# Attention by whole heads on 128 rows, and a first stage that alternates x and weights by K tile

## The chip, the cores and the metric

The kernel runs on one core of a Trainium2 chip. The metric is the device time of one execution in microseconds. A core has TensorE (PE: matmuls and transposes; its weight loads are listed apart as PEld), VectorE (DVE), ScalarE (ACT), GpSimd (POOL), SyncE (SP, which here only issues transfers), DMA queues that the engines issue into, an SBUF of 128 partitions and a PSUM of eight banks, each of 128 partitions by 512 floats, for matmul results.

## The reference

A decoder trunk of two layers on one sequence of 256 tokens, 2048 wide, everything in float32. Each layer projects the normed input to q, k, v (1024 columns each) and three 1024-column inputs of a gated convolution, runs differential attention over 8 heads beside the convolution, projects both back, and ends with a squared-ReLU MLP of 8192 columns.

```
for l in range(DEPTH):
    h = _rmsnorm(x, attn_norm_g[l])
    q, k, v, gate_b, gate_c, conv_in = jnp.split(h @ w_in[l], splits, axis=-1)
    q = _rmsnorm(q.reshape(B, S, N_HEADS, 2, HEAD_DK), q_norm_g[l])
    k = _rmsnorm(k.reshape(B, S, N_HEADS, 2, HEAD_DK), k_norm_g[l])
    ...
    s = jnp.einsum('bqhmd,bkhmd->bhmqk', q, k) * scale + bias
    s = jnp.where(dist >= 0, s, NEG)
    p = jax.nn.softmax(s, axis=-1)
    p = p[:, :, 0] - lam * p[:, :, 1]
    attn = jnp.einsum('bhqk,bkhd->bqhd', p, v)
    attn = (_rmsnorm(attn, subln_g[l]) * (1.0 - lam_init)).reshape(B, S, ATTN_WIDTH)
    conv = gate_b * _short_conv(gate_c * conv_in, conv_w[l])
    x = x + jnp.concatenate([attn, conv], axis=-1) @ w_out[l]
    hm = _rmsnorm(x, mlp_norm_g[l]) @ w_up[l]
    x = x + jnp.square(jax.nn.relu(hm)) @ w_down[l]
```

A head has two score maps (m = 0, 1), each over 64 of its 128 q and k columns. The maps are softmaxed apart and combined with a factor lambda.

## The kernel before

**Precision.** Every float32 matrix product is made of three products in the type fp32r: each operand is split into a rounded part `hi` and a rest `lo`, and `TERMS` (L38) lists hi x hi, hi x lo and lo x hi. The splits are made on ACT (`hi`, a copy that rounds) and DVE (`lo`, a subtraction). Transposes go through TensorE against an identity `ident`, in plain fp32.

**Stages.** A layer is a *mixer* (L602 to L664) and an *mlp* (L670 to L985). The tokens are two tiles t of 128. In the mixer come, for each half of the heads (four heads, 512 columns), three calls of `linear` (L328) named q, k and v; then eight calls of `linear_t` (L347) named gc and ci in turns, four named gb, and four calls of `linear` named o. `linear` runs over 16 K tiles (128 rows of weights each), with six matmuls of 128x128 by 512 columns a K tile (two token tiles by three terms). `linear_t` holds weights as the stationary operand. A group of four K tiles takes eight matmuls of 512 columns, activations' hi and lo side by side against the weights' hi, and eight of 256 against their lo.

**Weights.** `Weights` (L268) is a queue of jobs in program order. A job loads a piece of two K tiles (512 KB, issued on SP) into a `raw` tile, and `halves` rounds it: `whi` on ACT (L285), `wlo` on DVE (L286). There are four `raw` tiles and three pairs of rounded ones (`wpool`). `take` (L313) hands the next piece to TensorE and has made three jobs more by then (`AHEAD`). In layer 0 the first two pieces are rounded by K tile (`cut`). For layer 0, `first_loads` (L989) issues two weight loads ahead of each further part of x; the four parts of x are named x0 to x3 in what follows, each 512 columns of all 256 tokens, and the weight pieces w0, w1 and on. x0 is loaded in two halves at the very start (L146).

**Order of work.** TensorE's order is the program's, written out by hand (L116). The other engines' instructions are put in order by a scheduler when the kernel is built; only those given to `late` (L118) keep the program's order. Work beside the stages comes from `Background` (L55): generators that give a number with each yield, namely after how many ticks they go on. A tick is one K tile of `linear` (six matmuls of 512 columns), or four matmuls of 512 or four of 256 in `linear_t`. When a generator goes on, its TensorE instructions are put in TensorE's order at that place.

**Norms.** `Norm.chunk` (L397) transposes one of the four parts of x (16 transposes in two PSUM banks), multiplies by the gain and splits (`split_gained`, L249), marks the part ready, and squares x with a running sum. `Norm.factors` (L420) makes the row factors, which multiply the projections afterwards, and `across`, the same factors spread along columns by a matmul (`rbc`, L446), for the convolution. The generators of layer 0 are started at ticks 1, 5 and 9 of the first q pass; the first part is done ahead of it.

**q and k.** `qk_norm` (L458), started when a pass ends, squares and norms the result on ACT, DVE and POOL, waits 8 ticks (L477), transposes each token tile (four heads, a bank) and writes hi and lo of all heads in one ACT and one DVE instruction each (L484, L485), a tick apart.

**Attention.** `attention` (L489), started 3 ticks after a v pass, runs one `unit` for each token tile and head, tile 0 first, staggered by 4 ticks (L573). So attention of heads 0 to 3 runs beside the q pass of the second half, and that of heads 4 to 7 beside gc and ci. A unit makes two score maps, three matmuls each with 64 rows of contraction (L503) and 128 (t = 0) or 256 (t = 1) key columns; adds the bias and takes the maximum on DVE (L506); exponentials with sums on ACT (L513); combines the maps into `p` on DVE (L524); 9 ticks later transposes `p` (L529), splits it into `pT` (L531, L532); and 4 ticks later multiplies by v (L539, 3 or 6 matmuls of 128 columns) into one bank `av` for four heads. The last unit of a token tile copies that bank, norms it, waits 9 ticks (L562) and transposes it into `dst`, the input of o. `s` has three buffers, `p` and `pT` two each, in the pool `tmp` (L606).

**Bias.** `load_bias` (L230) starts at tick 10. In layer 0 it first runs `small_setup` (L199), which turns small vectors (loaded at L168 to L183 by POOL's queue) into gains and factors, and writes the biases by distance to DRAM; two 1 MB loads then read them back with a shift for each row (L238), and after 4 ticks (L241) eight ACT copies (L244) mirror them into `bias`. 

**Memory.** `nat` (L111) holds work tiles of 512 columns, seven of them; `bpool` (L608) holds eight tiles of 2048 columns: q, k and v parts, bias loads, attention and convolution outputs; `fill` (L131) is a tile that nothing uses, and sets where the ones behind it lie.

Of the kernel before, what the change touches and what calls it, by code (L numbers as in the profile page):

```python
# [15 lines left out]
P = 128  # L16
# [5 lines left out]
NH = 8  # L22
# [79 lines left out]
def trunk(ctx: ExitStack, tc: tile.TileContext, x, w_in, w_out, conv_w, q_norm_g, k_norm_g,  # L102
# [8 lines left out]
    nat = ctx.enter_context(tc.tile_pool(name="nat", bufs=7))  # L111
# [19 lines left out]
    const.tile([P, 40], F32, tag="fill", name="fill")  # L131
# [4 lines left out]
    def load_x(n, cuts=1):  # L136
        for c in range(cuts):
            lo, hi = c * CH // cuts, (c + 1) * CH // cuts
            nc.sync.dma_start(
                xs[n][:, :, lo:hi],  # L140
                x[0, :, n * CH + lo:n * CH + hi].rearrange("(t p) c -> p t c", p=P))
# [4 lines left out]
    load_x(0, 2)  # L146
# [3 lines left out]
    mhalf = const.tile([P, NH], F32, tag="mhalf", name="mhalf")  # L150
    nc.vector.memset(mhalf, -0.5)
# [16 lines left out]
    vec = const.tile([ROWS, P], F32, tag="vec", name="vec")  # L168
    nc.gpsimd.dma_start(vec[0:NCW, :], conv_w.rearrange("l i (k p) -> (l i k) p", p=P))
    for i, g in enumerate((q_norm_g, k_norm_g)):  # L170
        for m in range(2):
            nc.gpsimd.dma_start(
                vec[QG + i * DEPTH:QG + (i + 1) * DEPTH, m * DK:(m + 1) * DK], g)
    nc.gpsimd.dma_start(vec[QG + 2 * DEPTH:MG, :], subln_g)
    nc.gpsimd.dma_start(vec[MG:ROWS, :], mlp_norm_g.rearrange("l (k p) -> (l k) p", p=P))
    lamv = const.tile([1, 4, DEPTH, DK], F32, tag="lamv", name="lamv")
    for i, a in enumerate((lambda_q1, lambda_q2, lambda_k1, lambda_k2)):
        nc.gpsimd.dma_start(lamv[:, i], a[None])
    sel = const.tile([NB + 1, REL], F32, tag="sel", name="sel")
    nc.gpsimd.dma_start(sel, selector)  # L180
    rel = const.tile([NB + 1, 2 * NH], F32, tag="rel", name="rel")
    nc.vector.memset(rel[NB:NB + 1, :], NEG)
    nc.gpsimd.dma_start(rel[0:NB, :], rel_bias)  # L183
    ones = const.tile([P, P], F32, tag="ones", name="ones")
    nc.vector.memset(ones, 1.0)

# [12 lines left out]
    def small_setup():  # L199
# [27 lines left out]
        nc.vector.tensor_copy(nlam, lps[:, :DEPTH])  # L227


    def load_bias(l, bpool, bias):  # L230

        if l == 0:
            yield from small_setup()
# [154 lines left out]
    class Norm:  # L388
# [31 lines left out]
        def factors(self):  # L420
            while not all(t.ready for t in self.tiles):
                yield 1
# [607 lines left out]
```

## Time and profile before

| | |
|---|---|
| median of three runs | 2178.3 us (2177.54 to 2178.63) |
| the profiled execution | 2181.2 us, its span 2179.4 us |
| TensorE | 11066 instructions |
| VectorE | 2229 instructions |
| ScalarE | 1718 instructions |
| GpSimd | 194 instructions |
| read from HBM, written | 425.84 MB, 18.90 MB |
| MLP's share of the chain of waits | upc 29%, dn 15%, pr 13% |
| mixer's share | o 8%; q, k, v, gc, ci, gb 4% each; sc 1%, av 1% |

The page comes from one profiled execution. Busy time of an engine is the sum of its instructions without overlap; TensorE's matmuls are pipelined, so that the duration shown for one (0.39 us for 512 columns) is longer than the distance of two starts (0.227 us). In the chain of waits each step leads back from the end of the kernel to what released it, or to the instruction ahead of it on its engine. In a table by stretches each row has the stretch in us, its length, the busy time and instruction count of TensorE, its weight loads, VectorE, ScalarE and GpSimd, the TensorE clock that was granted (1.00 is full), the DMA engines' busy share, and GB/s. In rows of the timeline and of the chain come the start in us, the length, the engine, the source line, and the destination and sources by the program's names; `x6` is a run of six instructions, and square brackets hold the idle time ahead and what ended it.

### The profile page before, as it was taken

What the parts mean: (1) busy time and instruction counts of PE and PEld (TensorE: products, weight loads), DVE (VectorE), ACT (ScalarE), POOL (GpSimd) and SP (SyncE); (2) the same over time, 40 slices, a digit from 0 to 9 for tenths busy, and PEclk for the clock granted to TensorE, in tenths of its full rate; (3) what the DMA queues carried; (4) which work ended last, traced back from release to release, by engine and by line L of the source; (5) the groups of instructions that cost most, each with busy time, mean ns of one, the idle gap of its engine ahead of it and who ended that gap; (6) DMA issues with size and microseconds to landing.
All of it is one profiled execution on the core that took longest, in us unless ns stands there. A gap on an engine that the chain in (4) does not pass through costs nothing.

```text
span 2179.4 us, 29050 instructions
## 1 busy us (share of the span) xinstructions
PE 2156.3 (99%) x11066; PEld 1828.2 (84%) x11066; DVE 1604.7 (74%) x2229; ACT 1271.6 (58%) x1718; POOL 136.9 (6%) x194
## 2 busy tenths in 40 slices
PE   8999999999999999999999999999999999999999
PEld 6888888888888888888888888888888888888887
DVE  6677655698888888855566776557988888887554
ACT  6456445566666666644455664446666666665443
POOL 2021100000000000100011111000000000001000
PEclk9999999999999999999999999999999999999999
DMA  7545666476666666577565465656676666666774
GB/s 261 177 154 188 209 184 189 158 242 212 215 217 217 211 213 218 192 265 241 174 212 175 155 210 190 188 166 198 218 219 216 213 213 216 218 209 211 246 241 145
DMA packets 292491, 446.62 MB, mean 205 GB/s; under 512 B 10403, under 2 KB 191221, under 8 KB 292352
## 3 DMA queue, kind: packets, MB, share of 16 engines
q1 hardware_dynamic: 285648, 423.66, 61.4%
q0 software_dynamic: 6656, 21.10, 2.6%
q8 instruction: 86, 1.41, 0.3%
q14 instruction: 53, 0.43, 0.1%
q10 hardware_dynamic: 48, 0.02, 0.0%
HBM read 425.84 MB, written 18.90 MB: 204 GB/s over the span
## 4 chain that ended last, share of the span: by engine, by line
PE 94%; DVE 2%; DMA 2%; ACT 1%; issue 1%; SPq 0%; DVEq 0%; ACTq 0%
PE upc L812 29%; PE dn L972 15%; PE pr L852 13%; PE o L341 8%; PE q L341 4%; PE gc L363 4%; PE ci L363 4%; PE k L341 4%; PE gb L363 4%; PE v L341 4%; PE upw L812 1%; DMA uraw<-in_w_up_dram 1%; PE sc L503 1%; PE av L539 1%; DVE ulo L698 1%
## 5 line engine op out<-in xcount | busy, mean ns | idle before, releaser
L286 DVE TENSOR_TENSOR wlo<-raw,whi 128x1024 fp32r<-128x1024 f32 (+1 forms) x386 | 474.3, 1230 | 383.5 <-ACT whi L285 379.4
L285 ACT ACTIVATE whi<-raw 128x1024 fp32r<-128x1024 f32 (+1 forms) x386 | 406.8, 1055 | 477.6 <-PE dn L972 167.0
L812 PE MATMUL upc<-nT,uhi 128*128 128x512 f32 x1920 | 477.6, 391 | 0.0
L697 ACT ACTIVATE uhi<-uraw 128x1024 fp32r<-128x1024 f32 x256 | 271.0, 1060 | 285.7 <-PE upc L812 254.0
L812 PEld LDWEIGHTS upc<-nT,uhi 128*128 128x128 f32 x1920 | 352.8, 188 | 68.2
L698 DVE TENSOR_TENSOR ulo<-uraw,uhi 128x1024 fp32r<-128x1024 f32 x256 | 312.9, 1222 | 115.5 <-ACT uhi L697 113.1
L972 PE MATMUL dn<-whi,g 128*128 128x512 f32 x1024 | 316.4, 389 | 0.0
L812 PEld LDWEIGHTS upc<-nT,ulo 128*128 128x128 f32 x1920 | 261.9, 190 | 18.7
L812 PE MATMUL upc<-nT,ulo 128*128 128x256 f32 x1920 | 267.7, 282 | 0.0
L972 PEld LDWEIGHTS dn<-whi,g 128*128 128x128 f32 x1024 | 192.2, 188 | 39.7
L972 PE MATMUL dn<-wlo,g 128*128 128x512 f32 x512 | 199.7, 390 | 1.2 <-DVE wlo L286 1.0
L341 PE MATMUL o<-whi,cat 128*128 128x512 f32 x512 | 159.6, 390 | 0.0
L972 PEld LDWEIGHTS dn<-wlo,g 128*128 128x128 f32 x512 | 96.1, 188 | 22.9 <-DVE wlo L286 2.9
L341 PEld LDWEIGHTS o<-whi,cat 128*128 128x128 f32 x512 | 96.1, 188 | 19.8
L341 PE MATMUL o<-wlo,cat 128*128 128x512 f32 x256 | 99.6, 389 | 0.0
L834 POOL DMA_DIRECT2D hid<-h x64 | 35.0, 546 | 950.0 <-ACT h L833 914.1
L852 PE MATMUL pr<-t13h,f 128*128 128x512 f32 x240 | 93.8, 391 | 0.0
L341 PE MATMUL q<-whi,nT 128*128 128x512 f32 x256 | 86.2, 406 | 3.6 <-ACT nT L251 3.6
L341 PE MATMUL k<-whi,nT 128*128 128x512 f32 x256 | 85.3, 399 | 0.0
L852 PE MATMUL pr<-t24h,f 128*128 128x512 f32 x240 | 84.0, 391 | 0.0
L852 PE MATMUL pr<-b2h,f 128*128 128x512 f32 x240 | 84.0, 391 | 0.0
L341 PE MATMUL v<-whi,nT 128*128 128x512 f32 x256 | 83.4, 396 | 0.0
(330 smaller groups left out, 3428.5 us busy)
## 6 DMA issues: line engine op xcount, KB each, us to landing
uraw<-in_w_up_dram SPq DMA_DIRECT2D x128, 1024.0 KB, 5.9
raw<-in_w_in_dram SPq DMA_DIRECT2D x192, 512.0 KB, 3.9
draw<-in_w_down_dram SPq DMA_DIRECT2D x64, 1024.0 KB, 5.0
raw<-in_w_down_dram SPq DMA_DIRECT2D x64, 1024.0 KB, 5.3
raw<-in_w_out_dram SPq DMA_DIRECT2D x64, 512.0 KB, 3.6
hid<-h POOLq DMA_DIRECT2D x64, 256.0 KB, 4.3
back<-hid SPq DMA_DIRECT2D x32, 512.0 KB, 3.3
rev<-by_dist_d POOLq DMA_DIRECT2D x4, 1024.0 KB, 10.1
```

The source lines that it names most:

```text
L285: nc.scalar.activation(hi[:, k], raw[:, k], AF.Copy)
L286: nc.vector.tensor_sub(lo[:, k], raw[:, k], hi[:, k].bitcast(F32))
L341: nc.tensor.matmul(acc[:, t], a.ap[:, pa, k % KG, t * P:(t + 1) * P], (hi, lo)[pw][:, j], start=(k == 0 and n == 0), stop=(k == nk - 1 and ...
L363: nc.tensor.matmul(acc[:, f, 0] if part else acc[:, f], wt[:, k % 4, fs], a.ap[:, 0, k % KG] if part else a.ap[:, :, k % KG], start=(part ...
L503: nc.tensor.matmul(sc[:, :W], qT[m * DK:(m + 1) * DK, a, i, t * P:(t + 1) * P], kT[m * DK:(m + 1) * DK, b, i, :W], start=(n == 0), stop=(n ...
L539: nc.tensor.matmul(av[:, i * P:(i + 1) * P], pT[:, a, k * P:(k + 1) * P], v[:, b, k, i * P:(i + 1) * P], start=(k == 0 and n == 0), stop=( ...
L697: nc.scalar.activation(hi, src, AF.Copy)
L698: nc.vector.tensor_sub(lo, src, hi.bitcast(F32))
L812: nc.tensor.matmul(acc[:, 0] if part else acc, wt[:, k], a.ap[:, 0, k % KG] if part else a.ap[:, :, k % KG], start=(part == 0 and kh == 0 ...
L834: nc.gpsimd.dma_start(hid[i // 2][:, i % 2 * 2 * S:(i % 2 + 1) * 2 * S], u)
L852: nc.tensor.matmul(prods[n], fs[j][:, pa, a], b[pw], start=(j == 0 and m == 0), stop=(stop and m == 2))
L972: nc.tensor.matmul(acc[:, t], f[:, pa, k, t * P:(t + 1) * P], (hi, lo)[pw][:, k % 2], start=(b == 0 and k == 0 and m == 0), stop=(b == NB2 ...
```

## The change

**Attention.** A unit takes one head with both token tiles, and units are staggered by 8 ticks. Its two score maps go into two banks. Scores contract 128 rows: `q_parts` puts q's hi on a map's 64 rows and q's lo on the other 64; `k_parts` puts k's hi on both halves (`kT`) and k's lo on the map's rows with zeros on the others (`kL`, zeroed by POOL at the start of a mixer). One matmul with `kT` gives hi x hi + lo x hi, one with `kL` hi x lo. So a head has four matmuls of 128 columns and four of 256, all with 128 rows, where it had twelve with 64. The parts are written by 64-row halves: two ACT and two DVE instructions a token tile for q (one and one before), and four ACT and two DVE ones for k. The three blocks of a head's `p` are transposed one after the other, and `pT` hi multiplies v's hi and lo side by side (256 columns), `pT` lo v's hi (128 columns): six matmuls for nine. The halves of `av` are added, and the result squared, head by head. `s` holds both tiles (two buffers, and `p` is written in place of its first map); `pT` has one buffer. The waits are 10 ticks for 9 ahead of p's transposes, 12 for 9 ahead of the output's, 12 for 8 ahead of q's and k's.

**Start.** `begin` loads, on SP, half of x0 (256 KB), K tile 0 of w0 (256 KB), the other half of x0, K tile 1, then w1, x1, w2, w3, x2, x3. `Norm.begin` takes the K tiles of x0 one by one: two transposes, the split, and the rounding of that K tile's weights (of w0 and w1). TensorE runs matmuls of a tile of ones ahead of that, 11 at first and 3 after every second K tile, in plain fp32, whose result nothing reads. In layer 0 the squares of x1 and x2 come 10 and 8 ticks after their transposes, so the row factors (and `rbc`) come in the k pass. `take` makes one job ahead at first and up to three later, and the first roundings keep the program's order.

**Setup and bias.** The small vectors go to a tile of `bpool`, `setup_loads` issues them at the beginning of layer 0's mixer, and in layer 0 the bias copies wait 12 ticks for 4. `nat` has six tiles for seven, `fill` 48 columns for 40, and some small tiles have one buffer.

```
@@ -128,27 +128,36 @@
...
-    load_x(0, 2)
...
+    ones = const.tile([P, P], F32, tag="ones", name="ones")
+    nc.vector.memset(ones, 1.0)
...
+    def warm_up(n):
+
+        for _ in range(n):
+            nc.tensor.matmul(warm[:, 0, :P], ones, ones, start=True, stop=True)
...
     ident = const.tile([P, P], F32, tag="ident", name="ident")
     make_identity(nc, ident)
-    mhalf = const.tile([P, NH], F32, tag="mhalf", name="mhalf")
-    nc.vector.memset(mhalf, -0.5)
+    warm_up(11)
...
@@ -274,19 +289,42 @@
...
-            first = self.cut and i < 2
-            for k in (slice(0, 1), slice(1, None)) if first else (slice(None),):
-                nc.scalar.activation(hi[:, k], raw[:, k], AF.Copy)
-                nc.vector.tensor_sub(lo[:, k], raw[:, k], hi[:, k].bitcast(F32))
+            if not self.by_tile:
+                pair = (nc.scalar.activation(hi, raw, AF.Copy),
+                        nc.vector.tensor_sub(lo, raw, hi.bitcast(F32)))
+                if self.ramp and len(self.made) < 7:
+                    for ins in pair:
+                        late(ins)
...
+        def begin(self):
...
+            self.by_tile = self.ramp = True
+            raw = self.pool.tile([P, 2, CH], F32, tag="raw", name="raw", bufs=RAW)
+            w, row, c = self.first
+            for k in range(2):
+                load_x(0, k * CH // 2, (k + 1) * CH // 2)
+                nc.sync.dma_start(raw[:, k], w[row + k * P:row + (k + 1) * P, c:c + CH])
+            self.early.append(raw)
+            self.load_early(1)
+            raws = list(self.early)
+            self.made += [self.jobs[i]() for i in range(2)]
+            self.by_tile = False
+
+            def part(k):
+                (hi, lo), raw, j = self.made[k // 2], raws[k // 2], k % 2
+                late(nc.scalar.activation(hi[:, j], raw[:, j], AF.Copy))
+                late(nc.vector.tensor_sub(lo[:, j], raw[:, j], hi[:, j].bitcast(F32)))
+
+            return part
...
@@ -303,17 +341,20 @@
...
+            if not self.jobs:
+                self.first = w, row, c
...
-                self.early.append(self.jobs[len(self.early)].load())
+                self.early.append(self.jobs[len(self.made) + len(self.early)].load())
...
-            while len(self.made) < min(len(self.jobs), i + 1 + AHEAD):
+            ahead = min(AHEAD, max(1, i - 4)) if self.ramp else AHEAD
+            while len(self.made) < min(len(self.jobs), i + 1 + ahead):
...
@@ -410,6 +452,12 @@
...
+            if (self.which, self.l) == (0, 0) and n < D // CH - 1:
+                yield 12 - 2 * n
+            self.squares(n)
+
+        def squares(self, n):
+            self.squared += 1
...
@@ -417,10 +465,26 @@
...
+        def begin(self, part):
+
+            a = self.tiles[0].open()
+            for k in range(KG):
+                tp = ps.tile([P, CH], F32, tag="av", name="tpb3", bufs=1) if k == KG - 1 else bank(f"tpb{k}")
+                for t in range(NT):
+                    nc.tensor.transpose(tp[:, t * P:(t + 1) * P],
+                                        xs[0][:, t, k * P:(k + 1) * P], ident)
+                if k % 2:
+                    warm_up(3)
+                split_gained(a, k, tp[:, :S], norm_gain(0, 0, k))
+                part(k)
+            self.tiles[0].ready = True
+            self.squares(0)
+            yield 1
...
-            while not all(t.ready for t in self.tiles):
+            while self.squared < D // CH:
...
@@ -455,7 +519,33 @@
...
+    def q_parts(dst):
...
+        def put(tp3, gain, c):
+            for m, r in enumerate(HALF):
+                hi, lo = dst[r, m, :, c], dst[HALF[1 - m], m, :, c]
+                nc.scalar.activation(hi, tp3[r], AF.Copy, scale=gain[r])
+                nc.vector.scalar_tensor_tensor(lo, tp3[r], gain[r], hi.bitcast(F32),
+                                               op0=ALU.mult, op1=ALU.subtract)
+        return put
...
+    def k_parts(dst, low):
...
+        def put(tp3, gain, c):
+            for m, r in enumerate(HALF):
+                hi, lo = dst[r, m, :, c], low[r, m, :, c]
+                nc.scalar.activation(hi, tp3[r], AF.Copy, scale=gain[r])
+                nc.vector.scalar_tensor_tensor(lo, tp3[r], gain[r], hi.bitcast(F32),
+                                               op0=ALU.mult, op1=ALU.subtract)
+                nc.scalar.activation(dst[HALF[1 - m], m, :, c], tp3[r], AF.Copy, scale=gain[r])
+        return put
...
@@ -474,103 +564,117 @@
...
-        yield 8
+        yield 12
...
-            for m in range(2):
-                sc = bank(f"sc{h}_{t}_{m}")
-                for n, (a, b) in enumerate(TERMS):
-                    nc.tensor.matmul(
-                        sc[:, :W], qT[m * DK:(m + 1) * DK, a, i, t * P:(t + 1) * P],
-                        kT[m * DK:(m + 1) * DK, b, i, :W], start=(n == 0), stop=(n == 2))
...
+            s = tmp.tile([P, 2, 3 * P], F32, tag="s", name=f"s{h}", bufs=2)
...
+            sc = [bank(f"sc{h}_{m}") for m in range(2)]
+            for flip in range(2):
+                for k in (kT, kL):
+                    for t in range(NT):
+                        W, m = (t + 1) * P, t ^ flip
+                        nc.tensor.matmul(
+                            sc[m][:, OFF[t]:OFF[t] + W], qT[:, m, i, t * P:(t + 1) * P],
+                            k[:, m, i, :W], start=(k is kT), stop=(k is kL))
...
-            yield 9
...
+            p = s[:, 0]
...
+            yield 10
+            tp = bank(f"ptp{h}")
+            for b in range(3):
...
+            pT = tmp.tile([P, 2, 3 * P], F32R, tag="pT", name=f"pT{h}", bufs=1)
...
+            av = ps.tile([P, CH], F32, tag="av", name=f"av{h}", bufs=1)
+            av = av.rearrange("p (t n c) -> p t n c", t=NT, n=2)
+            for t in range(NT):
+                for k in range(t + 1):
+                    w = slice(OFF[t] + k * P, OFF[t] + (k + 1) * P)
+                    nc.tensor.matmul(av[:, t], pT[:, 0, w], v[:, :, k, i * P:(i + 1) * P],
+                                     start=(k == 0), stop=False, skip_group_check=True)
+                    nc.tensor.matmul(av[:, t, 0], pT[:, 1, w], v[:, 0, k, i * P:(i + 1) * P],
+                                     start=False, stop=(k == t), skip_group_check=True)
+            mine = slice(i * P, (i + 1) * P)
+            nc.scalar.activation(ao[:, :, mine], av[:, :, 1], AF.Copy)
+            nc.vector.tensor_add(ao[:, :, mine], av[:, :, 0], ao[:, :, mine])
+            for t in range(NT):
+                nc.scalar.activation(s[:, 1, t * P:(t + 1) * P], ao[:, t, mine], AF.Square,
+                                     accum_out=ss[:, i, t:t + 1])
...
-            yield 9
...
-        yield from staggered([unit(t, i) for t in range(NT) for i in range(4)], 4)
...
+            yield 12
...
+        yield from staggered([unit(i) for i in range(4)], 8)
...
@@ -621,19 +727,22 @@
...
+            kL = biasp.tile([P, 2, 4, S], F32R, tag="kL", name=f"kL{l}")
+            for m, r in enumerate(HALF):
+                nc.gpsimd.memset(kL[HALF[1 - m], m].bitcast(F32), 0.0)
...
@@ -987,12 +1096,14 @@
     norm = Norm(0, 0)
 
     def first_loads(weights):
+        part = weights.begin()
         for n in range(1, D // CH):
-            weights.load_early(2)
             load_x(n)
+            if n == 1:
+                weights.load_early(2)
             work.start(norm.chunk(n, 2), 4 * n - 3)
-
-    work.start(norm.chunk(0, 0))
+        work.start(norm.begin(part))
+
     for l in range(DEPTH):
         mnorm = mixer(l, norm, first_loads if l == 0 else lambda weights: None)
         norm = mlp(l, mnorm, l == DEPTH - 1)
```

225 lines of the change are left out of this document (112 added, 113 removed).

## The prediction, made before the changed kernel ran

> **What bounds the kernel now.** I read the page's busy line and its chain of waits first, then the table by stretches, to see where TensorE is not busy.
>
> ```profile
> span 2179.4 us, 29050 instructions
> PE 2156.3 (99%) x11066; PEld 1828.2 (84%) x11066; DVE 1604.7 (74%) x2229; ACT 1271.6 (58%) x1718; POOL 136.9 (6%) x194
> PE 94%; DVE 2%; DMA 2%; ACT 1%; issue 1%; SPq 0%; DVEq 0%; ACTq 0%
> ...
> 0.00:15.00 15.00, 7.89 (x27) 5.98 (x28) 5.79 (x13) 7.42 (x15) 7.45 (x19) 1.00 0.88 307
> 165.00:215.00 50.00, 50.00 (x327) 43.38 (x326) 40.15 (x110) 32.68 (x81) 8.53 (x13) 1.00 0.54 175
> ```
>
> TensorE carries 94% of the chain and has no idle time where attention runs (165 to 215 us: 50.00 of 50.00; the columns are length, busy time of PE, PEld, DVE, ACT, POOL, granted clock, DMA share, GB/s). So matmul time taken out there shortens the kernel one for one, as long as nothing else comes late. Of TensorE's 23 us of idle time 7.1 lie in the first 15 us. VectorE is busy for 40 of the 50 us of that stretch: the cover there is thin.
>
> **Scores on 128 rows.** A block of six 64-row matmuls is priced from the start of the plain matmul before it to the start of the second plain one after it, less two plain steps, so that what it costs on its edges is counted. A plain 512-column step is 10.90 / 48 = 0.227 us.
>
> ```profile
> 38.43 10.90 PE k L341 x48
> ...
> 87.55 0.39 PE L341 MATMUL q<-whi,nT 128*128 128x512 f32 x1
> 87.86 0.56 PE L503 MATMUL sc<-kT,qT 64*128 64x128 f32 x6
> 88.35 0.50 PE L341 MATMUL q<-whi,nT 128*128 128x512 f32 x1
> 88.69 0.39 PE L341 MATMUL q<-wlo,nT 128*128 128x512 f32 x1
> ...
> 112.79 0.39 PE L341 MATMUL k<-whi,nT 128*128 128x512 f32 x1
> 113.10 0.62 PE L503 MATMUL sc<-kT,qT 64*128 64x256 f32 x6
> 113.66 0.50 PE L341 MATMUL k<-whi,nT 128*128 128x512 f32 x1
> 114.00 0.40 PE L341 MATMUL k<-wlo,nT 128*128 128x512 f32 x1
> ```
>
> The 128-column block costs 1.14 - 0.45 = 0.69 us, the 256-column block 1.21 - 0.45 = 0.76: 1.45 a head. Each loses some 0.2 us on its edges (0.31 going in and 0.34 coming out against 0.227). No score on 128 rows is in the trace. The nearest rows are the 128-row products of probabilities and v, and a linear pass of which half the matmuls are 512 and half 256 columns wide.
>
> ```profile
> 49.33 0.44 PE q00tp L481 x4
> ...
> 136.25 0.78 PE L539 MATMUL av<-v,pT 128*128 128x128 f32 x6
> 136.87 0.41 PE L529 MATMUL ptp<-ident,p 128*128 128x128 f32 x2
> 137.03 0.48 PE L341 MATMUL v<-whi,nT 128*128 128x512 f32 x1
> 137.34 0.39 PE L341 MATMUL v<-wlo,nT 128*128 128x512 f32 x1
> ...
> 156.63 0.78 PE L539 MATMUL av<-v,pT 128*128 128x128 f32 x6
> 157.25 0.44 PE L341 MATMUL v<-whi,nT 128*128 128x512 f32 x1
> 157.53 0.40 PE L341 MATMUL v<-wlo,nT 128*128 128x512 f32 x1
> ...
> 264.62 44.69 PE gb L363 x256
> ```
>
> Six 128-column matmuls alone cost 157.53 - 156.63 - 0.227 = 0.67: 0.103 each and 0.05 at the end. A 256-column one costs (44.69 - 128 x 0.227) / 128 = 0.122. Eight, four of each width, come to 0.67 + 2 x 0.103 + 4 x 0.019 = 0.95. Gain 0.50 a head, 16 heads: **7.9 us**. Bounds: 4.7 if the 0.2 us on the edges is not due to the 64 rows and stays with the one block (0.30 a head); 10 if the narrow matmuls fall to the 64-row block's 0.08 (0.49 / 6).
>
> Against this edit speaks the Trainium skill, TensorEngine Tiling (Array Packing), Performance Considerations: a contraction of 64 lets two row tiles work at the same time. By that alone the old twelve would take half their streams, an estimated 0.55 us a head, and the change would cost 0.4 a head. Its Key Properties say as well that changing the tiling mode drains the array, and the edges of 0.31 and 0.34 agree; measured with drains and all, the old two blocks take 1.45.
>
> **Products with v, and transposes.** Six products and two transposes cost 137.34 - 136.25 - 0.227 = 0.86. The other tile's three and one are 0.86 - 3 x 0.103 - 0.11 (a transpose, 0.44 / 4) = 0.44. So 1.30 a head. After, three products of 256 columns and three of 128 take 0.67 + 3 x 0.019 = 0.73, and three transposes, now a block by themselves, 0.33 with 0.08 at the end (137.34 - 137.03 - 0.227): 1.14. Gain 0.16 a head, **2.6 us** (bounds 1 and 4: all or none of the edges). Attention together: 10.5.
>
> **The start.**
>
> ```profile
> 1.72 6.02 DMA raw<-in_w_in_dram
> 3.75 1.97 PE L405 MATMUL tpn<-ident,x 128*128 128x128 f32 x8
> 9.32 0.80 PE L341 MATMUL q<-whi,nT 128*128 128x512 f32 x1 [3.60 <-ACT nT L251]
> 10.34 1.05 PE L341 MATMUL q<-whi,nT 128*128 128x512 f32 x2
> 11.19 0.63 PE L341 MATMUL q<-wlo,nT 128*128 128x512 f32 x1
> 14.18 0.41 PE L341 MATMUL q<-whi,nT 128*128 128x512 f32 x1
> 14.43 1.03 PE L405 MATMUL tpn<-ident,x 128*128 128x128 f32 x8
> ```
>
> The first q matmul waits for 512 KB of weights (landed at 7.74), then for two roundings and a split on ACT. Until about 14.2 us a matmul takes 0.43 (two from 10.34 to 11.19), so twelve lose 12 x 0.2 = 2.4 us, though the granted clock reads 1.00. After, x and weights alternate by 256 KB: the same bytes in SP's queue, with x1 one issue later; both of K tile 0 are there near 5 (the first x before 3.75, 512 KB more of weights by 7.74), K tile 1 near 7.7. Then TensorE itself decides: 11 warm-ups from about 1.0 us, each two fp32 passes of 0.25 (1.97 / 8) at the slow rate; the gains' transpose; eight transposes and six warm-ups, in program order. Before needed TensorE active from 9.32 to 14.2, 4.9 us, for the fast rate; from 1.0 that comes near 5.9, with ten warm-ups done. The last (0.26), gains (0.2), eight transposes (8 x 0.13, from 1.03 / 8) and six warm-ups (6 x 0.26) end near 9.0. So q begins 0.3 earlier and at 0.227 a step: 0.3 + 2.4. Against it: a chunk's transposes now stand one K tile ahead of their use, not two, and weights are rounded one job ahead at first, so that splits and roundings meet on ACT: -0.2. Together **2.5 us**. Bounds: -1 (warm-ups slow to the end: 11 + 6 of them 0.5 each, q near 10.5 and no fast rate) and 4.5 (fast from 4 us on, nothing late). TensorE: Matmul & The Clock Gate (the Trainium skill), Part 1, puts the fast rate about 4 us into sustained matmuls; the 4.9 here is near it, and by 4 this term would be 0.4 larger.
>
> Small loads into another tile, bias copies 8 ticks later, kL's zeroing on GpSimd, one `nat` buffer less, the fill: costed at nothing. ACT has 17 and GpSimd 41 free of 50 us in the stretch above, and the bias is not read before the first scores (87.86). Were it late, that wait comes once, 1 us at most.
>
> **What comes late.** ACT now writes k in eight 64-row pieces instead of two of 128 rows, equally long by columns.
>
> ```profile
> 150.87 0.69 ACT L484 ACTIVATE kT<-k01tp,gains 128x512 fp32r<-128x512 f32 x1
> 156.83 1.06 ACT L285 ACTIVATE whi<-raw 128x1024 fp32r<-128x1024 f32 x1 [1.68 <-PE v L341]
> ...
> 184.02 0.63 PE L503 MATMUL sc<-kT,qT 64*128 64x256 f32 x6
> 189.51 0.48 DVE L524 SCALAR_TENSOR_TENSOR p<-s,c 128x256 f32<-128x256 f32 x1
> 193.81 0.41 PE L529 MATMUL ptp<-ident,p 128*128 128x128 f32 x2
> ```
>
> For heads 4 to 7 TensorE's order puts the scores behind two blocks of k's transposes, four K tiles of v (24 matmuls) and 8 + 4 of gc: 2 x 0.5 + 24 x 0.227 + 8 x 0.227 + 4 x 0.122 = 8.8 us. ACT's order in that time is whi (1.06), two k pieces (the second waits for its transposes, to 3.0), whi (which waits until TensorE frees a buffer, to 4.8), four pieces at 0.6 (7.2), whi, v's first tile, the last two pieces: 10.0. TensorE waits 1.2, once a layer: **-2.4** (bounds 0 and -4). Behind it stand all of gc, and whi, which needs TensorE's buffers. For heads 0 to 3 three K tiles of q stand in gc's place and the window is 10.6: hidden.
>
> Then a head's chain: four score reductions, four exponentials and two sums, where a tile had half of each. Before, p was ready at 189.99 for transposes at 193.81: 6.0 us after its scores, 3.8 to spare. After, between a head's scores and its transposes lie 10 ticks of 0.7 and some 2 us of other blocks, 9 us; the chain grows from 6 to about 8.5 (another 2 x 0.5 on DVE, 2 x 0.5 on ACT, 0.5 for p), and the third head's `s` has to wait for the first's squares, since there are two buffers. I count 0.2 us three times a layer, **-1.2** (bounds 0 and -10). In q, k and v ticks are twice as long: hidden.
>
> Sum: 10.5 + 2.5 - 2.4 - 1.2 = 9.4. The profiled execution took 2181.2 (1.8 beside its span), 2.9 above the median of 2178.3: 2171.8 on its own clock, **2168.9** against the median.
>
> **Rivals.** (a) Nothing comes late: 2168.9 - 3.6 = 2165.3. For it: ACT is free for 17 of 50 us. Against: whi is tied to TensorE's pace, so free time isn't where it is needed. (b) Reductions, sums and roundings on VectorE become the bound in the gc and ci stretch: eight heads each wait 1.2 more, 9.6: 2178.5. DVE's 40 of 50 us speak for it; that its work by head hardly grows, against. (c) Slower: TensorE waits for p ahead of its transposes in that stretch. The gain without this wait is 10.6, 1.3 for each of the eight heads; it decides once the chain takes 10.4 us and not 8.5. At a wait of 2.5, 20 us, the time is 2178.3 - 10.6 + 20 = 2187.7. The 3.8 to spare before speak against. (d) The start doesn't do what it is named for, with q late and slow: 3.5 worse, 2172.4. The 0.25 us passes speak for it.
>
> **How the numbers follow.** Forecast 0.52, (a) 0.24, (b) 0.11, (c) 0.05, (d) 0.08. The range goes from 2161 (the scores' and the start's upper bounds with nothing late) to 2176 (half of b). 0.2% is 4.4 us, about what a measurement of this kernel tells from no change, so faster is below 2173.9: nearly all of the forecast (0.50), (a), and 0.05 of (d), 0.79. Same 0.15, slower 0.06.
>
> **What would show it.** A score block of eight near 0.95 us with no 0.31 ahead of it; q's first matmul near 9.0, at 0.23 a step from there; k's first near 35.5; one wait of TensorE for kT in each layer, near 1.2. A wait for p or `s` above 1 us a head, or q's matmuls still at 0.43 after 10 us, would prove me wrong.

## The result, and the profile after

| | |
|---|---|
| changed kernel, median of 6 runs | 2168.8 us (2167.6 to 2170.6) |
| kernel before, median of 6 runs | 2178.4 us (2177.5 to 2179.4) |
| ratio | 0.9953, 95% interval 0.9943 to 0.9964 |
| forecast | 2168.9 us, range 2161 to 2176 |
| the profiled execution | 2167.6 us, its span 2165.8 us |

The change gains 9.6 us, as forecast. First the page of the changed kernel: span, busy times, and the chain by engine.

```profile
span 2165.8 us, 28903 instructions
PE 2146.9 (99%) x10988; PEld 1828.7 (84%) x10988; DVE 1612.4 (74%) x2197; ACT 1294.1 (60%) x1743; POOL 135.3 (6%) x178
PE 92%; DVE 3%; DMA 2%; ACT 2%; issue 1%; SPq 0%; DVEq 0%; ACTq 0%
```

TensorE is still the bound, but its share of the chain has gone down by two points, to DVE and ACT. The stretches that answer to those of before:

```profile
0.00:15.00 15.00, 13.95 (x76) 12.63 (x77) 6.35 (x15) 8.44 (x18) 9.33 (x21) 1.00 0.86 298
165.00:215.00 50.00, 49.41 (x308) 43.79 (x307) 38.40 (x88) 32.40 (x80) 7.31 (x8) 1.00 0.68 219
```

The first has 13.95 us of TensorE for 7.89, warm-ups among them. In the second, without a gap before, TensorE now misses 0.6 us. The view of waits (engine, line, what was waited for: us in total, times, longest) says for what:

```profile
PE sc L594 <- ACT kT L545: 4.1, 2, 2.0
PE pr L961 <- DVE f L953: 2.3, 3, 1.0
PE atp L667 <- DVE an L658: 1.6, 2, 1.0
```

The wait for `kT` was forecast (2.4), that for `an`, ahead of the transposes of attention's output, was not.

To see where time comes and goes, take the start of the first matmul of each pass in the timeline, and subtract that of before (us; negative is earlier):

| pass | layer 0 | layer 1 |
|---|---|---|
| first q | -0.8 | -7.4 |
| first k | -3.2 | -7.4 |
| first v | -2.8 | -7.4 |
| second q | -2.8 | -7.4 |
| second v | -5.3 | -9.8 |
| first gc | -6.5 | -11.0 |
| first ci | -4.8 | -9.3 |
| third gc, and on to o | -6.1 | -10.1 |
| dn | -7.2 | -13.2 |

The start brings 2.8 (the 0.4 between k and v is `rbc`, which moved from the q pass into the k pass). Heads 0 to 3, beside the second q, k and v, bring 3.7 and 3.6; heads 4 to 7 give 0.4 of it back in layer 0, and 0.8 in layer 1. Up to the last pass of the second mixer that is 6.1 and 2.7, together 8.8. The two profiled executions differ by another 4.8 us in the MLPs, whose program the change leaves as it was. Each lies off its median the other way (2181.2 against 2178.4, 2167.6 against 2168.8), which is 4.0 together. So most of these 4.8 us are execution against execution, and start and attention have 8.8 by the trace and 9.6 by the medians.

A score block, then the transposes of `p`, then products with v, in the timeline:

```profile
84.77 0.39 PE L382 MATMUL q<-whi,nT 128*128 128x512 f32 x1
85.00 0.39 PE L594 MATMUL sc<-kT,qT 128*128 128x128 f32 x2
85.23 0.40 PE L594 MATMUL sc<-kL,qT 128*128 128x128 f32 x2
85.46 0.39 PE L594 MATMUL sc<-kT,qT 128*128 128x128 f32 x2
85.69 0.39 PE L594 MATMUL sc<-kL,qT 128*128 128x128 f32 x2
85.92 0.39 PE L382 MATMUL q<-whi,nT 128*128 128x512 f32 x1
86.15 0.40 PE L382 MATMUL q<-wlo,nT 128*128 128x512 f32 x1
...
100.27 0.39 PE L382 MATMUL q<-whi,nT 128*128 128x512 f32 x1
100.50 0.49 PE L625 MATMUL ptp<-ident,s 128*128 128x128 f32 x3
100.74 0.48 PE L382 MATMUL q<-whi,nT 128*128 128x512 f32 x1
101.06 0.39 PE L382 MATMUL q<-wlo,nT 128*128 128x512 f32 x1
...
106.07 0.39 PE L382 MATMUL k<-whi,nT 128*128 128x512 f32 x1
106.29 0.28 PE L636 MATMUL av<-v,pT 128*128 128x256 f32 x1
106.93 0.45 PE L382 MATMUL k<-whi,nT 128*128 128x512 f32 x1
107.22 0.39 PE L382 MATMUL k<-wlo,nT 128*128 128x512 f32 x1
```

By the prediction's price, the scores of a head cost 86.15 - 84.77 - 0.45 = 0.93 us for 1.45, and the step into the block is a plain one (85.00 - 84.77 = 0.23 for 0.31). Transposes cost 101.06 - 100.27 - 0.45 = 0.34, products 107.22 - 106.07 - 0.45 = 0.70, together 1.04 for 1.30. Over 16 heads: 8.3 and 4.2.

### The profile page after: what moved, and what is told of

Same layout as the page of the kernel before. It is cut to its first block, busy times and chain, and to the rows that moved or that the text cites. A ratio compares the mean times of both kernels' runs of the same rounds, so it can differ in the third digit from the quotient of the medians.

```text
span 2165.8 us, 28903 instructions
## 1 busy us (share of the span) xinstructions
PE 2146.9 (99%) x10988; PEld 1828.7 (84%) x10988; DVE 1612.4 (74%) x2197; ACT 1294.1 (60%) x1743; POOL 135.3 (6%) x178
## 4 chain that ended last, share of the span: by engine, by line
PE 92%; DVE 3%; DMA 2%; ACT 2%; issue 1%; SPq 0%; DVEq 0%; ACTq 0%
PE upc L921 29%; PE dn L1081 16%; PE pr L961 13%; PE o L382 8%; PE gb L404 4%; PE k L382 4%; PE v L382 4%; PE ci L404 4%; PE q L382 4%; PE gc L404 3%; DMA raw<-in_w_in_dram 1%; PE upw L921 1%; PE sc L594 1%; DMA back<-hid 1%; DVE ulo L807 1%
## 5 line engine op out<-in xcount | busy, mean ns | idle before, releaser
L299 DVE TENSOR_TENSOR wlo<-raw,whi 128x1024 fp32r<-128x1024 f32 x382 | 468.9, 1229 | 364.1 <-ACT whi L298 363.3
L298 ACT ACTIVATE whi<-raw 128x1024 fp32r<-128x1024 f32 x382 | 404.6, 1060 | 448.9 <-PE dn L1081 167.8
```

What stands on the lines that cost most here:

```text
L298: pair = (nc.scalar.activation(hi, raw, AF.Copy), nc.vector.tensor_sub(lo, raw, hi.bitcast(F32)))
L299: nc.vector.tensor_sub(lo, raw, hi.bitcast(F32)))
```

## Experiments

Each time is the median, and each ratio is taken against the kernel before on the same chip. What each was expected to show was written ahead of its run. The kernel before had 2178.4 us beside the changed kernel and 2178.8 to 2179.5 beside the runs below. So where a text says how far a run lies from the changed kernel, about 1 us of it can be the chip.

**Start alone, attention alone, first try.** The attention of before in the changed kernel, and the changed attention (with the setup tile, six `nat` tiles and the longer bias wait) in the kernel before.

```
-    def attention(l, qT, kT, kL, v, h0, dst, bias, tmp):
+    def attention(l, qT, kT, v, h0, dst, bias, tmp):
...
```

> The changed kernel with the attention of the kernel before (units by tile and head, 64-row scores); start, setup and bias as changed. Theory (the two parts add): the first q matmul starts near 8.5 us, k's first near 35.1 and v's near 58.2, 3.2 and 2.8 earlier than before, and everything behind v stays 2.8 earlier, except what the first MLP steps do; about 2175.5 against 2178.4. Rival (the 4 us by which the two profiled executions differ inside the MLPs belong to the start or to the buffers changed with it): about 2171.5. Rival (the start buys nothing unless attention follows it): 2178.

> The kernel before with the changed attention (and the setup tile in the other pool, the bias wait and six work tiles, without which it doesn't fit). Theory: q's first matmul at 9.3 and v's at 61.0 as before; gains of 0.53 a head in scores and 0.25 in products and transposes, 12.5 in all; waits of TensorE for kT, 2.2 a layer, and for an, 0.8 to 1.4 a layer; net 6.0: about 2172.4. Rival (the 4 us inside the MLPs belong to attention): 2168.4. Rival (the waits are made by the earlier start, and not there without it): 2166.

2196.8 us (ratio 1.0078, 1.0066 to 1.0091) and 2198.5 (1.0085, 1.0071 to 1.0099): 17 and 19 slower than before, and 19 and 26 above the slowest that was expected. The time went in o and dn, whose matmuls took 0.234 us from start to start for 0.227. Other small tiles leave other addresses behind them: in the kernel before and in the changed one all pools of matmul operands begin at a multiple of 512 bytes; here the mixer's and MLP's begin 224 or 32 bytes past one, and in attn_only the others 448 past one. As trials of the parts these two settle nothing.

**Addresses alone.** The changed kernel with one unused tile more.

```
     work = Background()
+
+    small.tile([P, 56], F32, tag="pad", name="pad", bufs=1)
```

> The changed kernel, not an instruction of it different, with one unused tile of 224 bytes ahead of the mixer's and MLP's pools, so that these lie 224 bytes off a multiple of 512. Theory: o, dn and upc matmuls go from 0.227 to about 0.234 us as in start_only, some 20 us: 2186 to 2192, and with that the width of the unused tiles, costed at nothing in the prediction, is worth more than the whole change. Rival (start_only and attn_only were slow for what they leave undone): 2168.8.

2187.6 us (1.0037, 1.0024 to 1.0051), 18.9 above the changed kernel. The chain of waits of the changed kernel, and then that of this one (start, us, what, number of instructions):

```profile
328.58 21.78 PE o L382 x96
...
948.66 130.58 PE dn L1081 x576
```

```profile
329.20 22.39 PE o L384 x96
...
953.35 134.39 PE dn L1083 x576
```

The same 96 matmuls take 22.39 for 21.78 (0.233 each for 0.227), the same 576 take 134.39 for 130.58. Nothing waits there in either. Of their operands, those loaded as weights (`cat`, `g`) have moved, and the moving ones (`whi`, `wlo`) have not.

**The parts again, aligned.** Both with unused columns (and attention with one buffer for one small tile) until their pools lie at multiples of 512 bytes.

```
+    small.tile([P, 72], F32, tag="pad", name="pad", bufs=1)
...
-    const.tile([P, 40], F32, tag="fill", name="fill")
+    const.tile([P, 56], F32, tag="fill", name="fill")
```

> The start alone again, as in start_only, with one unused tile of 288 bytes more ahead of the mixer's and MLP's pools, so that all tiles of matmul operands lie at multiples of 512 bytes, as in both the kernel before and the changed one (in start_only those pools lay 224 bytes off). Theory (where the tiles lie made start_only slow: matmuls of o and dn took 0.234 us for 0.227): they are back at 0.227, v's first matmul stays 2.8 earlier than before and everything behind it too, about 2175.5. Rival (the start alone costs something else): 2190 or more.

> The attention alone again, as in attn_only, with tiles at multiples of 512 bytes. Theory: o and dn at 0.227; 12.5 less for the blocks, 4.5 for kT and 2 for an: net 6.0, about 2172.4. Rival (the waits come from the earlier start): 2166. Rival (the attention alone costs something else): 2190 or more.

Attention alone: 2172.7 us (0.9971, 0.9960 to 0.9982), 6.2 faster, close to the theory's number. `kT` makes TensorE wait 4.0 there as well, so that wait doesn't come from the earlier start. But in this trace the granted clock is 0.50 for 3.4 us behind each of the two waits, and from gc's first matmul to ci's it takes 18.0 us for 16.5 in the changed kernel. That loss of 3.0 was not in the theory, so the agreement is partly chance. The start alone: 2179.5 (1.0002, 0.9993 to 1.0011), nothing gained. Its k pass begins 3.9 earlier, its v pass 0.5 later than before. The waits and the stretches of this run (length, then busy times of the five engines, granted clock, DMA share, GB/s):

```profile
PE q00tp L547 <- DVE q00n L538: 2.2, 1, 2.2
```

```profile
48.00:50.00 2.00, 0.08 (x1) 0.08 (x2) 1.83 (x4) 0.00 (x0) 0.23 (x1) 0.97 0.57 152
50.00:52.00 2.00, 2.00 (x7) 1.81 (x8) 0.21 (x1) 0.93 (x2) 0.00 (x0) 0.50 0.60 214
52.00:54.00 2.00, 2.00 (x7) 1.57 (x7) 0.55 (x1) 1.20 (x3) 0.00 (x0) 0.68 0.01 3
54.00:56.00 2.00, 2.00 (x10) 1.63 (x10) 1.23 (x1) 0.66 (x1) 0.00 (x0) 1.00 0.00 0
```

The row factors now come in the k pass, and q's normed rows wait for them. Eight ticks after the pass they aren't there. After 2.5 us from one matmul's start to the next, 2.2 of them idle, the granted clock is 0.50, and matmuls take 0.427 us until 53.3. The k pass takes 27.1 us, and 23.2 in the next run, which has no such wait: the wait of 2.2 costs 4.0.

**The start alone with q's and k's transposes at 12 ticks.**

```
-        yield 8
+        yield 12
```

> The start alone, aligned as in start_al, with q's and k's transposes 12 ticks after their pass, where it had 8. Theory (start_al lost its gain because the row factors now come in the k pass, so that q's normed rows weren't ready at 8 ticks: a wait of 2.2 us, after which TensorE ran at 0.427 us a matmul for some 3 us, granted clock 0.50): no wait there, v's first matmul 2.8 earlier than before and all behind it, 2175.5. Rival (transposes at 12 ticks make kT late for the 64-row scores as well): a wait at the first scores of heads 4 to 7, 2177 to 2179. Rival (the start's gain is taken back behind v in any case): 2179.

2176.4 us (0.9986, 0.9977 to 0.9995): 3.1 faster than before, with none of these waits. So the 12 ticks, which the prediction took for a part of attention's timing, are a condition of the start. Start 3.1 and attention 6.2 make 9.3, against 9.6 for both together; since attention's trial holds the clock's loss, this says that the two parts add, but not to better than some 3 us.

**64 rows again.** Scores of the merged unit with twelve 64-row matmuls in one block; q and k written by one ACT and one DVE instruction a token tile.

```
-                            sc[m][:, OFF[t]:OFF[t] + W], qT[:, m, i, t * P:(t + 1) * P],
-                            k[:, m, i, :W], start=(k is kT), stop=(k is kL))
+                            sc[m][:, OFF[t]:OFF[t] + W], qT[r, a, i, t * P:(t + 1) * P],
+                            kT[r, b, i, :W], start=(n == 0), stop=(n == 2))
```

> The changed kernel with scores on 64 rows again, twelve matmuls of a head in one block; q and k written by one ACT and one DVE instruction a token tile as before. Theory (the cost is in the 64-row matmuls and at their edges; the eight pieces of k on ACT are what makes kT late): a block costs 1.25 to 1.45 against 0.92, that is 5 to 8 us lost over 16 heads, and the wait for kT, 4.5 in both layers, goes: 0.5 to 4 slower than the changed kernel, 2169 to 2173. Rival (only the edges of two blocks cost, so that one block of 64 rows is as cheap): block near 0.95, and without the wait 2164.5. Rival (kT is late by the longer stagger and not by its pieces): the wait stays, 2174 to 2177.

2171.1 us (0.9961, 0.9948 to 0.9973), 2.4 above the changed kernel (1.4 when each is compared with the kernel before beside it). The timeline:

```profile
84.06 0.39 PE L382 MATMUL q<-whi,nT 128*128 128x512 f32 x1
84.38 1.24 PE L581 MATMUL sc<-kT,qT 64*128 64x128 f32 x12
85.55 0.50 PE L382 MATMUL q<-whi,nT 128*128 128x512 f32 x1
85.88 0.39 PE L382 MATMUL q<-wlo,nT 128*128 128x512 f32 x1
```

The block costs 85.88 - 84.06 - 0.45 = 1.37: merging two blocks saved 0.08 of 1.45, so the loss is in the 64-row matmuls and at their edges (84.38 - 84.06 = 0.32 going in, 0.33 coming out), not in having two blocks. That is 0.44 a head, 7.0 in all. The wait for `kT`, which costs 4.4, is gone, and so is that for `an`, which costs 2.0 (below). So 128 rows buy 7.0 and pay about 6.4 for it in waits; on their own they bring little, and the next runs show how to have the 7.0 without the waits.

**k's transposes sooner.**

```
-        yield 12
+        yield wait
...
+                work.start(qk_norm(acc, r, k_parts(kT, kL), k_gain[:, l:l + 1], f"k{l}{half}", 8))
```

> The changed kernel with k's transposes 8 ticks after its pass, where it has 12 (q's stay at 12). Theory (kT is late because ACT gets to its eight pieces too late): the pieces start four ticks, 5.5 us, earlier, the wait of 2.2 a layer goes and nothing takes its place: 4.4 faster than the changed kernel, 2164.4. Rival (ACT has no room there: the pieces push the weights' roundings back, and TensorE waits for those): within 1 us of the changed kernel, 2168. Rival (k's normed rows are not ready at 8 ticks with more work beside them): a wait of some 2 us at k's transposes, 2168 to 2171.

2163.7 us (0.9927, 0.9913 to 0.9941), 5.1 below the changed kernel. The wait for `kT` is gone in both layers. One of 1.4 for k's normed rows comes in the first half of layer 0, where the row factors are late, and one of the two waits for `an` is left (1.0).

**What makes `an` late.** In the changed kernel, SP's queue, ACT, DVE and TensorE at the end of layer 0's attention (in brackets the idle time ahead and what ended it):

```profile
187.32 3.54 SPq L799 DMA_DIRECT2D uraw<-in_w_up_dram  x3
190.96 14.04 SPq L339 DMA_DIRECT2D raw<-in_w_in_dram  x5
...
202.29 1.06 ACT L298 ACTIVATE whi<-raw 128x1024 fp32r<-128x1024 f32 x1 [3.34 <-DMA raw<-in_w_in_dram]
...
203.38 1.22 DVE L299 TENSOR_TENSOR wlo<-raw,whi 128x1024 fp32r<-128x1024 f32 x1 [3.74 <-ACT whi L298]
204.52 1.28 DVE L658 TENSOR_TENSOR an<-ao,af 128x512 f32<-128x512 f32 x2
...
205.26 0.66 PE L667 MATMUL atp<-ident,an 128*128 128x128 f32 x4 [0.59 <-DVE an L658]
```

The MLP's first three loads, 1 MB each, go where `bias` and `kL` lay. The last reductions of scores, which read `bias`, end at 187.1 us (193.5 before), and the loads are issued at 187.3 (205.5 before). The weight piece issued at 190.96 lands only 11.2 us later (4.0 at the median), ACT stands idle for 3.3, `wlo` comes late, and `an` is behind it on DVE. To test it, the two pools change places, and those loads stand five pieces further back:

```
+            tmp = scope.enter_context(tc.tile_pool(name="tmp", bufs=3))
             biasp = scope.enter_context(tc.tile_pool(name="biasp", bufs=1))
-            tmp = scope.enter_context(tc.tile_pool(name="tmp", bufs=3))
```

> The changed kernel with the two pools of attention opened in the other order, so that the memory into which the MLP's first three 1 MB weight loads go comes free later, and they stand five weight loads further back in SP's queue. Theory (TensorE waits for an, 0.8 and 1.2 us, because whi waits for a weight piece that lands 8 us late behind those 3 MB, and an stands behind wlo on DVE): the piece lands in time and the wait goes: 2 faster than the changed kernel, 2166.8. Rival (an is late by its own chain of squares and powers on ACT and POOL): the wait stays, 2168.8. Rival (the 3 MB meet the next weight pieces instead): the wait moves by some ten us and stays, 2168.8.

2167.2 us (0.9947, 0.9935 to 0.9960), 1.6 below the changed kernel, and no wait for `an`. By medians alone 1.6 is near what can be told. The traces show it at the place: from the first gc to the third, layer 0 takes 57.34 us in the changed kernel and 56.55 here, layer 1 57.80 and 56.55. So the two waits, 1.6 us of idle time, cost 0.8 and 1.2, together 2.0.

**Both mended.** k's transposes at 8 ticks (12 in the first half of layer 0), pools as in swap.

```
+    ... f"k{l}{half}", 8 if l or half else 12))
```

> The changed kernel with k's transposes 8 ticks after their pass (12 only in the first half of layer 0, whose row factors come late), and with the pools in the order of swap. Theory (the three waits are separate terms): kT's 4.5 goes and an's 2 goes, k00tp's 1.4 of the run with 8 ticks throughout doesn't come: about 6.5 faster than the changed kernel, 2162. Rival (ACT's pieces, moved earlier, make another wait, as the 1.0 for an that stayed with 8 ticks): 2163.7, no better than with 8 ticks alone.

2162.0 us (0.9920, 0.9906 to 0.9933): 6.8 below the changed kernel, 17.5 below before in its own comparison, faster than both. TensorE waits for neither `kT` nor `an`; its longest wait is 1.1, in the MLP.

**Without warm-ups.**

```
-    warm_up(11)
...
-                    warm_up(3)
+                    warm_up(0)
```

> The changed kernel without its matmuls of ones: nothing else computed is left out. Theory (transposes can start once x0's first half is there at 3.9 us, at the slow rate, and q once w0's K tile 0 is rounded): q's first matmul near 6, at 0.427 a matmul until near 11, K tile 1 done near 11 as with warm-ups, since its weights land at 7.85 anyway: within 1 of the changed kernel, 2168.3 to 2169.8. Rival (the fast rate from the first q matmul on is all that the start gains): twelve slow matmuls, 2.4 lost, 2171.2. Rival (TensorE's pauses for x and weights keep it slow still longer, to 15 us or more): 2172 or more.

2169.8 us (0.9954, 0.9941 to 0.9966), 1.0 above, and as far below the kernel before beside it as the changed kernel (9.7 and 9.6). By the medians alone that is no difference. In the trace q starts at 7.1 (not 6), 1.4 sooner than with warm-ups, but at 0.427 a matmul until 12.4, and its pass ends 0.65 later, against a gain of 2.8 for the whole start. So most of that gain comes from the order of loads and roundings, not from the matmuls of ones. Behind both waits for `kT` the granted clock falls to 0.50 in this trace, as in attn_al.

**p's transposes two ticks sooner.**

```
-            yield 10
+            yield 8
```

> The changed kernel with p's transposes 8 ticks after the scores, where it has 10: two ticks, some 1.4 us, less beside gc and ci. Theory (the chain from scores to p takes 9.6 us there, not the 8.5 forecast, and p is ready only 0.25 to 1.0 us ahead of its transposes): heads 4 to 7 wait 0.4, 1.1, 0.4 and 1.0 us, some 3 a layer: 2174 to 2175. Rival (ACT and DVE put p's work off only because nothing needs it sooner, and their planned order brings it forward): no wait above 0.5, 2168 to 2169.5.

2170.2 us (0.9960, 0.9947 to 0.9974), 1.4 above, between the two expectations: eight waits for p, 3.2 us in all and 0.6 at most, while the waits for `kT` shrink to 2.1 and those for `an` to 0.2, since the planned order of the other engines changes with it.

## Why the prediction was right, by its own steps

| term | forecast | measured |
|---|---|---|
| scores on 128 rows | 7.9 | 8.3 |
| products and transposes | 2.6 | 4.2 |
| start | 2.5 | 2.8 in the trace, 3.1 alone |
| wait for `kT` | -2.4 | -4.4 |
| chain of p and `s` | -1.2 | 0 |
| wait for `an` | not there | -2.0 |
| sum | 9.4 | 8.9 (2.8 for the start); pass starts 8.8, medians 9.6 |

The waits stand with what they cost from start to start, which is more than their idle time (4.1 and 1.6). The time is right partly by luck, because misses cancel: 2 us more from the blocks and 1.2 not lost on p, against 2 more for `kT` and 2 for `an`.

*Scores.* The price of 0.95 a head, from 128-row products, was 0.02 off. The Trainium skill's rule against it (TensorEngine Tiling (Array Packing), Performance Considerations: two 64-row tiles at work at the same time) isn't put to the test here. Twelve 64-row matmuls in one block take 1.37 us, eight of 128 rows 0.93; but before and in that run all six of one map, on the same 64 rows, stand ahead of the other map's six. Matmuls that alternate between the two halves of the rows were not tried, so whether those would be cheaper still stays open.

*Products and transposes.* The three transposes take 0.34, where 0.33 and an edge of 0.08 were counted, the six products 0.70 for 0.73: 1.04 a head for 1.14. The edge was taken over from the old blocks. With it gone, the gain of 4.2 lies just past the bound of 4.

*Start.* The timeline of the changed kernel:

```profile
1.05 5.07 PE L156 MATMUL warm<-ones 128*128 128x128 f32 x22 [1.05 <-DVE mhalf L148]
...
7.45 0.60 PE L474 MATMUL tpb<-ident,x 128*128 128x128 f32 x4
7.89 0.83 PE L156 MATMUL warm<-ones 128*128 128x128 f32 x6
8.48 0.48 PE L382 MATMUL q<-whi,nT 128*128 128x512 f32 x1
8.79 0.39 PE L382 MATMUL q<-wlo,nT 128*128 128x512 f32 x1
9.03 0.62 PE L382 MATMUL q<-whi,nT 128*128 128x512 f32 x2
9.49 0.40 PE L382 MATMUL q<-wlo,nT 128*128 128x512 f32 x1
```

The 22 passes of the first eleven warm-ups end near 6.0, 0.23 us each on the mean (0.25 was assumed). From 7.45 on four transposes take 0.44, so the fast rate is there, as forecast for about 5.9; the trace's record of the clock begins with 1.00 at 6.3. (In the kernel before that record begins at 14.2, so the 1.00 in the row of its first 15 us says nothing of the time up to there.) The price of 4.9 us of activity was read from one trace, and that it fits is partly luck: in the ten traces with these warm-ups the clock is full from 4.2 (start_only) to 6.8 (p8), and q starts between 7.6 and 8.7. q starts at 8.5 (9.0 forecast) and steps at 0.23 (9.03 to 9.49 for two); k's first matmul is at 35.05 (35.5). What the step overlooked is that putting off the squares makes the row factors late for q's transposes; the 12 ticks hid it.

*Wait for `kT`.* Mechanism right, size too small. ACT's order in the changed kernel:

```profile
150.18 1.06 ACT L298 ACTIVATE whi<-raw 128x1024 fp32r<-128x1024 f32 x1 [1.68 <-PE v L382]
151.15 0.67 ACT L542 ACTIVATE kT<-k01tp,gains 64x512 fp32r<-64x512 f32 x1
152.40 0.68 ACT L542 ACTIVATE kT<-k01tp,gains 64x512 fp32r<-64x512 f32 x1 [0.58 <-PE k01tp L571]
153.84 1.06 ACT L298 ACTIVATE whi<-raw 128x1024 fp32r<-128x1024 f32 x1 [0.76 <-PE v L382]
154.92 0.68 ACT L545 ACTIVATE kT<-k01tp,gains 64x512 fp32r<-64x512 f32 x1
...
157.75 1.06 ACT L298 ACTIVATE whi<-raw 128x1024 fp32r<-128x1024 f32 x1
158.83 0.69 ACT L749 ACTIVATE v<-v,rowf 128x512 fp32r<-128x512 f32 x1
159.55 1.26 ACT L545 ACTIVATE kT<-k01tp,gains 64x512 fp32r<-64x512 f32 x2
```

It is the order that was forecast, piece by piece. But a piece takes 0.70 us from start to start, where 0.6 was used for the last six: 0.6 of the 1.0 that is missing in a layer. The 128-row write of before, quoted in the prediction, took 0.69. The rest is spread over small terms: counted from the first transposes of k at 149.93, ACT is done at 10.9 us for 10.0, and TensorE reaches the scores at 8.7 for 8.8.

*Chain of p.* No wait, but hardly by a margin: in the changed kernel head 5's scores begin at 168.2, p is ready at 177.9 and its transposes start at 178.1. The chain takes 9.6 us, not 8.5, and the window 9.9, not 9; the other three heads of that stretch come to 8.5 to 8.8, the wait for `kT` taken off. Rival (c) was to decide from 10.4 on; the tightest head had 0.25 us left.

*What was missed.* "Small loads ..., the fill: costed at nothing" holds for the changed kernel because its unused columns keep all tiles at multiples of 512 bytes; shift shows that 18.9 us hang on it, twice the gain. And the loads that the earlier end of attention sets free (the three of 1 MB) were not followed to where they collide, which is the wait for `an`. 

*Rivals.* (b) didn't come: in the gc and ci stretch TensorE waits for `kT` and `an` alone. (d) fell with q at 8.5 us. (a), nothing late, is what the kernel with both waits mended shows: 2162.0, 3.3 below the 2165.3 worked out for it, 2.0 of it since the blocks cost less than forecast.

## What to carry to other kernels

When work on the bound engine is taken out, price the blocks from the trace, but then follow what ends sooner: which waits lose their cover, and which transfers are set free by memory that empties earlier. Two parts that each carry a condition of the other (here 12 ticks and the alignment of the pools) can't be tried alone until the condition is carried along. After an edit to small tiles, look at the step of an untouched pass before looking at anything else.

## What was not expected of the hardware

A displacement of 224 bytes for operands loaded as weights makes a 512-column matmul take 0.233 us for 0.227 in o and dn alike. Which boundary below 512 bytes an address has to keep wasn't tried by itself. In attn_only q's two operands both lie 448 bytes past a multiple of 512, by the sizes of the tiles, and its step stays at 0.227. 448 is a multiple of 64, and 224 and 32 are not, so a boundary of 64 bytes would fit these runs; so would a rule on the distance between the two operands, which is unchanged there.

The granted clock can fall after a wait of about 2 us, and the length of the wait alone doesn't decide it. In the aligned start 2.55 us from one matmul to the next (47.37 to 49.92) brought it down to 0.50. In start_only the same wait, 2.56 us (47.52 to 50.08), left it at 1.00. The wait for `kT`, 2.24 to 2.27 us, brought it down in both layers of attn_al and of warm0 and in layer 1 of shift, and left it at 1.00 in layer 0 of shift and in the changed kernel. The stretches behind the wait, first in start_only, then in attn_al (columns as in the stretches above):

```profile
50.00:52.00 2.00, 1.92 (x11) 1.66 (x12) 0.53 (x2) 1.23 (x3) 0.00 (x0) 1.00 0.65 228
162.00:164.00 2.00, 1.90 (x9) 1.90 (x10) 0.41 (x4) 1.79 (x3) 0.00 (x0) 0.52 0.74 241
```

What decides it in these traces is where the wait falls. Up to the end of the kernel, each slow stretch lasts 3.41 us, and the clock changes only at whole multiples of 3.41 us after it first was full (in the aligned start full at 5.51, slow from 49.88 to 53.30). Cut into steps of that length, the fourteen traces have eleven steps in which TensorE stood idle for 1.9 us or more, and the clock fell behind each of them; it fell behind no other, the nearest being 1.8 us idle (layer 0 of shift). So a wait of about 2 us costs another 1.5 us or nothing, as it falls into one step or across two. The Trainium skill (TensorE: Matmul & The Clock Gate, Part 1) puts the slow state after an idle window of about 3.4 us; here less was enough, and the measurement decides.
